# A batch norm over 32 images: tiles of half the columns in six buffers, and loads and stores that wait for their buffer alone

## The chip, the cores and the metric

The kernel runs on one core of a Trainium2 chip. The core has engines that compute, each with its own stream of instructions (here VectorE, called DVE in the profile, and ScalarE, called ACT), an engine that issues transfers (SyncE, called SP), and 16 DMA engines that move data between the chip's memory (HBM) and the core's own memory (SBUF, 128 partitions). The metric is the time of one execution on the device in microseconds (us); lower is better.

## The reference

The input x has the shape 32 x 256 x 128 x 128 (images, channels, height, width) in float32, 537 MB. The four parameters have one number per channel.

```python
def reference(x, gamma, beta, running_mean, running_var):
    eps = 1e-5
    mean = running_mean.reshape(1, -1, 1, 1)
    var = running_var.reshape(1, -1, 1, 1)
    gamma = gamma.reshape(1, -1, 1, 1)
    beta = beta.reshape(1, -1, 1, 1)
    return gamma * (x - mean) / np.sqrt(var + eps) + beta
```

Per channel this is one multiplication and one addition for every element: out = scale * x + shift, with scale = gamma / sqrt(var + eps) and shift = beta - mean * scale.

## The kernel before

The 256 channels are two blocks of 128, one channel to a partition. A tile is one image and one channel block: 128 partitions x 16384 columns (HW), 64 KB in each partition, 8.39 MB in all. There are 64 tiles (NT), and the list `order` (L84) takes all images of the first channel block and then all of the second. Three buffers `t0` to `t2` (NBUF) hold a tile each; tile i uses buffer i mod 3, and the result is written over the input in the same buffer.

**Start.** SP issues the left half of tile 0 (L87, semaphore `early`), the four parameter rows (L90), the right half of tile 0 (L94) and tiles 1 and 2 (L96). VectorE transposes the parameter rows so that each channel's number lies in its own partition (L107, L112), and ScalarE and VectorE work out `scale_t` and `shift_t` (L114 to L124).

**Loads.** For tiles 3 to 63 SP waits until the tile that had the buffer is stored (L102), and then for one more thing: `vdone` must have reached 2(i - 1) + 1, which is when VectorE has done the first small part of tile i - 1. That second wait (L104) is attached to the load itself (L103). So at most one load is in flight, since VectorE's first part waits for tile i - 1 to land.

**Compute.** VectorE takes the columns up to VCOLS = 14336 with one instruction `tensor_scalar` per part (L129): first STEP = 2560 columns, whose end lets the next load go, and then the other 11776. ScalarE takes the last 2048 columns with an `activation` (L140). For the last tile the border is VLAST = 9216.

**Stores.** ScalarE's stream has, for each tile, a wait for VectorE's two parts of it, then its own part, which also waits until the store of the tile before has ended, and then the store of the whole tile, issued from ACT's DMA queue (L153) once its own part is done (`adone`). So one store is in flight at a time.

At the end SP waits for the last stores and clears the semaphores (L171, L172).

Of the kernel before, what the change touches and what calls it, by code (L numbers as in the profile page):

```python
# [6 lines left out]


NBUF = 3
PAD = 936  # L10


STEP = 2560
VCOLS = 14336
VLAST = 9216


@with_exitstack
def kernel(
    ctx: ExitStack,  # L20
    tc: tile.TileContext,
    x: bass.AP,
    gamma: bass.AP,
    beta: bass.AP,
    running_mean: bass.AP,
    running_var: bass.AP,
    out: bass.AP,
):
    nc = tc.nc
    eps = 1e-5  # L30
    f32 = mybir.dt.float32

    N, C, H, W = x.shape
    P = nc.NUM_PARTITIONS
    assert C % P == 0
    NCB = C // P
    HW = H * W
    NT = N * NCB
    B = 32
    NQ = P // B  # L40
    NE = 16
    NPAR = 4

    xr = x.rearrange("n (cb p) h w -> (n cb) p (h w)", p=P)
    outr = out.rearrange("n (cb p) h w -> (n cb) p (h w)", p=P)

    def tile_of(name, *shape):
        return nc.alloc_sbuf_tensor(name, list(shape), f32)

    rows = tile_of("rows", B, NPAR * C)  # L50
    turned = tile_of("turned", B, NPAR * C)
    par = tile_of("par", P, NPAR, NCB)
    eps_t = tile_of("eps_t", P, 1)
    std_t = tile_of("std_t", P, NCB)
    rstd_t = tile_of("rstd_t", P, NCB)
    scale_t = tile_of("scale_t", P, NCB)
    ms_t = tile_of("ms_t", P, NCB)
    shift_t = tile_of("shift_t", P, NCB)
    tile_of("pad", P, PAD)
    bufs = [tile_of(f"t{s}", P, HW) for s in range(NBUF)]  # L60

    names = [f"loaded{s}" for s in range(NBUF)] + [f"stored{s}" for s in range(NBUF)]
    names += ["early", "vdone", "adone", "fetched", "vec", "act"]
    sems = {name: nc.alloc_semaphore(name) for name in names}
    loaded = [sems[f"loaded{s}"] for s in range(NBUF)]
    stored = [sems[f"stored{s}"] for s in range(NBUF)]
    early, vdone, adone, fetched, vec, act = (sems[n] for n in names[2 * NBUF :])
    used = range(min(s.num for s in sems.values()), max(s.num for s in sems.values()) + 1)
    assert len(used) == len(sems)

    count = [0]

    def step(inst, sem=None, value=None):
        if sem is not None:
            inst._wait_ge(sem, value)
        elif count[0]:
            inst._wait_ge(vec, count[0])
        inst.then_inc(vec, 1)
        count[0] += 1
        return count[0]  # L80

    left, right = slice(0, HW // 2), slice(HW // 2, HW)
    last = NT - 1
    order = [n * NCB + cb for cb in range(NCB) for n in range(N)]  # L84

    with tc.tile_critical():  # L86
        nc.sync.dma_start(out=bufs[0][:, left], in_=xr[order[0]][:, left]).then_inc(early, 16)  # L87
        zeroed = step(nc.vector.memset(rows[:], 0.0))  # L88
        for r, ap in enumerate((running_var, gamma, beta, running_mean)):
            inst = nc.sync.dma_start(out=rows[0:NE, r * C : (r + 1) * C], in_=ap.partition_broadcast(NE))  # L90
            if r == 0:
                inst._wait_ge(vec, zeroed)
            inst.then_inc(fetched, 16)
        nc.sync.dma_start(out=bufs[0][:, right], in_=xr[order[0]][:, right]).then_inc(loaded[0], 16)  # L94
        for i in range(1, NBUF):
            nc.sync.dma_start(out=bufs[i][:], in_=xr[order[i]]).then_inc(loaded[i], 16)  # L96
    tc.close()
    tc.compile()  # L98

    for i in range(NBUF, NT):  # L100
        s, turn = i % NBUF, i // NBUF
        nc.sync.wait_ge(stored[s], 16 * turn)  # L102
        inst = nc.sync.dma_start(out=bufs[s][:], in_=xr[order[i]]).then_inc(loaded[s], 16)  # L103
        inst._wait_ge(vdone, 2 * (i - 1) + 1)  # L104

    step(nc.vector.memset(eps_t[:], eps))  # L106
    step(nc.vector.transpose(out=turned[:], in_=rows[:]), fetched, 16 * NPAR)  # L107

    blocks = turned[:].rearrange("p (rc q b) -> p rc q b", q=NQ, b=B)
    flat = par[:].rearrange("p r cb -> p (r cb)")  # L110
    for q in range(NQ):
        placed = step(nc.vector.tensor_copy(out=flat[q * B : (q + 1) * B], in_=blocks[:, :, q, 0]))  # L112
    var_t, gamma_t, beta_t, mean_t = (par[:, r] for r in range(NPAR))
    nc.scalar.activation(  # L114
        out=std_t[:],
        in_=var_t,
        func=mybir.ActivationFunctionType.Sqrt,
        bias=eps_t[:],
        scale=1.0,
    )._wait_ge(vec, placed).then_inc(act, 1)  # L120
    step(nc.vector.reciprocal(out=rstd_t[:], in_=std_t[:]), act, 1)  # L121
    step(nc.vector.tensor_mul(out=scale_t[:], in0=gamma_t, in1=rstd_t[:]))  # L122
    step(nc.vector.tensor_mul(out=ms_t[:], in0=mean_t, in1=scale_t[:]))  # L123
    ready = step(nc.vector.tensor_sub(out=shift_t[:], in0=beta_t, in1=ms_t[:]))  # L124
    nc.vector.wait_ge(vec, ready)

    def vector_part(i, first, end):
        t, cb = bufs[i % NBUF], order[i] % NCB
        return nc.vector.tensor_scalar(  # L129
            out=t[:, first:end],  # L130
            in0=t[:, first:end],
            scalar1=scale_t[:, cb : cb + 1],
            scalar2=shift_t[:, cb : cb + 1],
            op0=mybir.AluOpType.mult,
            op1=mybir.AluOpType.add,
        ).then_inc(vdone, 1)

    def scalar_part(i, first):
        t, cb = bufs[i % NBUF], order[i] % NCB
        return nc.scalar.activation(  # L140
            out=t[:, first:],
            in_=t[:, first:],
            func=mybir.ActivationFunctionType.Identity,
            bias=shift_t[:, cb : cb + 1],
            scale=scale_t[:, cb : cb + 1],
        ).then_inc(adone, 1)

    def landed(i):
        return loaded[i % NBUF], 16 * (i // NBUF + 1)

    def store(i):
        s = i % NBUF
        nc.scalar.dma_start(out=outr[order[i]], in_=bufs[s][:])._wait_ge(adone, i + 1).then_inc(stored[s], 16)  # L153

    vector_part(0, 0, HW // 2)._wait_ge(early, 16)
    vector_part(0, HW // 2, VCOLS)._wait_ge(*landed(0))
    for i in range(1, NT):
        vector_part(i, 0, STEP)._wait_ge(*landed(i))
        vector_part(i, STEP, VLAST if i == last else VCOLS)
    for i in range(last):  # L160
        nc.scalar.wait_ge(vdone, 2 * (i + 1))
        inst = scalar_part(i, VCOLS)
        if i:
            inst._wait_ge(stored[(i - 1) % NBUF], 16 * ((i - 1) // NBUF + 1))
        store(i)
    scalar_part(last, VLAST)._wait_ge(*landed(last))
    nc.scalar.wait_ge(vdone, 2 * NT)
    store(last)

    for s in range(NBUF):  # L170
        nc.sync.wait_ge(stored[s], 16 * ((NT - s + NBUF - 1) // NBUF))  # L171
    nc.sync.sem_clear(used)  # L172
# [30 lines left out]
```

## Time and profile before

| what | value |
|---|---|
| time, median of 3 runs | 2481.03 us (2480.61 to 2481.18) |
| the profiled execution's own time | 2480.81 us |
| its span in the profile | 2479.5 us |
| VectorE busy | 508.7 us, 139 instructions |
| ScalarE busy | 139.8 us, 66 instructions |
| moved to and from HBM | 536.94 MB read, 536.87 MB written, 433 GB/s over the span |
| a tile's load, issue to landing (median) | 37.0 us |
| a tile's store, issue to landing (median) | 36.5 us |
| VectorE, 11776 columns / 2560 columns | 6406 ns / 1612 ns |
| ScalarE, 2048 columns | 2092 ns |

The span is the time from the first to the last instruction that the profiler recorded; the execution's own time has a little around it. Busy time is the sum of an engine's instruction durations. A DMA is a transfer; it is cut into packets, and each packet runs on one of the 16 DMA engines. Queue q1 carries SP's transfers (loads), q10 those of ACT (stores). The share of the DMA engines is the sum of the packets' durations over 16 engines and the length of the stretch, where a packet is counted in the stretch in which it starts; in a very short stretch the share is therefore far above 1.

### The profile page before, as it was taken

What the parts mean: (1) busy time and instruction counts of PE and PEld (TensorE: products, weight loads), DVE (VectorE), ACT (ScalarE), POOL (GpSimd) and SP (SyncE); (2) the same over time, 40 slices, a digit from 0 to 9 for tenths busy, and PEclk for the clock granted to TensorE, in tenths of its full rate; (3) what the DMA queues carried; (4) which work ended last, traced back from release to release, by engine and by line L of the source; (5) the groups of instructions that cost most, each with busy time, mean ns of one, the idle gap of its engine ahead of it and who ended that gap; (6) DMA issues with size and microseconds to landing.
All of it is one profiled execution on the core that took longest, in us unless ns stands there. A gap on an engine that the chain in (4) does not pass through costs nothing.

```text
span 2479.5 us, 514 instructions
## 1 busy us (share of the span) xinstructions
DVE 508.7 (21%) x139; ACT 139.8 (6%) x66; POOL 0.2 (0%) x4
## 2 busy tenths in 40 slices
DVE  2122121221212212122121221212212122121220
ACT  0000000000000000000000000000000000000001
POOL 0000000000000000000000000000000000000000
DMA  9999999999999999999999999999999999999999
GB/s 412 435 438 427 437 438 429 436 438 429 435 438 430 435 439 430 433 438 433 431 438 432 432 438 432 432 438 432 432 438 433 431 438 433 431 438 435 430 438 410
DMA packets 18708, 1073.85 MB, mean 433 GB/s; under 512 B 2128, under 2 KB 2192, under 8 KB 2192
## 3 DMA queue, kind: packets, MB, share of 16 engines
q1 hardware_dynamic: 9488, 536.94, 50.1%
q10 hardware_dynamic: 9216, 536.88, 50.0%
q14 instruction: 4, 0.03, 0.0%
HBM read 536.94 MB, written 536.87 MB: 433 GB/s over the span
## 4 chain that ended last, share of the span: by engine, by line
DMA 92%; DVE 4%; another core or an unknown queue 2%; ACT 0%; issue 0%; SPq 0%; DVEq 0%
DMA t<-in_x_dram 92%; DVE t L129 4%; ACT t L140 0%; SPq L90 0%; DVE rows L88 0%; DVEq L98 0%; SPq L86 0%
## 5 line engine op out<-in xcount | busy, mean ns | idle before, releaser
L129 DVE TENSOR_SCALAR t<-t,scale_t,shift_t 128x11776 f32<-128x11776 f32 (+2 forms) x128 | 505.2, 3989 | 1928.4 <-DMA t<-in_x_dram 1928.3
L140 ACT ACTIVATE t<-t,shift_t,scale_t 128x2048 f32<-128x2048 f32 x64 | 138.2, 2159 | 2297.3 <-DMA out_dram<-t 2274.5
L107 DVE STREAM_TRANSPOSE turned<-rows 32x1024 f32<-32x1024 f32 x1 | 1.2, 1232 | 7.6 <-DMA rows<-in_running_mean_dram 7.6
L114 ACT ACT_TABLE_LOAD x1 | 1.3, 1283 | 6.4 <-PEq L98 6.4
L88 DVE MEMSET rows<- 32x1024 f32 x1 | 0.9, 912 | 1.2 <-SPq L86 1.2
L106 DVE MEMSET eps_t<- 128x1 f32 x1 | 0.1, 59 | 4.4 <-PEq L98 4.4
L114 ACT ACTIVATE std_t<-par,eps_t 128x2 f32<-128x2 f32 x1 | 0.3, 295 | 8.5 <-DVE par L112 8.5
L112 DVE COPY par<-turned 32x8 f32<-32x8 f32 x4 | 0.7, 162 | 0.1
L121 DVE RECIPROCAL rstd_t<-std_t 128x2 f32<-128x2 f32 x1 | 0.2, 165 | 0.4 <-ACT std_t L114 0.4
L122 DVE TENSOR_TENSOR scale_t<-par,rstd_t 128x2 f32<-128x2 f32 x1 | 0.2, 161 | 0.0
L123 DVE TENSOR_TENSOR ms_t<-par,scale_t 128x2 f32<-128x2 f32 x1 | 0.2, 161 | 0.0
L124 DVE TENSOR_TENSOR shift_t<-par,ms_t 128x2 f32<-128x2 f32 x1 | 0.2, 160 | 0.0
L187 POOL MEMSET const-bfloat16-1.0<- 128x1 bf16 x1 | 0.1, 101 | 0.0
L187 POOL MEMSET const-uint8-127<- 128x1 uint8 x1 | 0.1, 101 | 0.0
L187 POOL MEMSET const-float32-0.0<- 128x1 f32 x1 | 0.1, 98 | 0.2 <-issue 0.2
L187 POOL MEMSET const-float32-1.0<- 128x1 f32 x1 | 0.1, 98 | 0.0
## 6 DMA issues: line engine op xcount, KB each, us to landing
t<-in_x_dram SPq DMA_DIRECT2D x2, 4096.0 KB, 16.0
out_dram<-t ACTq DMA_DIRECT2D x64, 36.5
t<-in_x_dram SPq DMA_DIRECT2D x63, 37.0
rows<-in_running_var_dram SPq DMA_DIRECT2D x1, 16.0 KB, 11.2
rows<-in_gamma_dram SPq DMA_DIRECT2D x1, 16.0 KB, 11.0
rows<-in_beta_dram SPq DMA_DIRECT2D x1, 16.0 KB, 10.7
rows<-in_running_mean_dram SPq DMA_DIRECT2D x1, 16.0 KB, 10.7
```

Of the source, the lines that this page charges most:

```text
L88: zeroed = step(nc.vector.memset(rows[:], 0.0))
L106: step(nc.vector.memset(eps_t[:], eps))
L107: step(nc.vector.transpose(out=turned[:], in_=rows[:]), fetched, 16 * NPAR)
L112: placed = step(nc.vector.tensor_copy(out=flat[q * B : (q + 1) * B], in_=blocks[:, :, q, 0]))
L114: nc.scalar.activation(out=std_t[:], in_=var_t, func=mybir.ActivationFunctionType.Sqrt, bias=eps_t[:], scale=1.0,)._wait_ge(vec, placed).t ...
L121: step(nc.vector.reciprocal(out=rstd_t[:], in_=std_t[:]), act, 1)
L122: step(nc.vector.tensor_mul(out=scale_t[:], in0=gamma_t, in1=rstd_t[:]))
L123: step(nc.vector.tensor_mul(out=ms_t[:], in0=mean_t, in1=scale_t[:]))
L124: ready = step(nc.vector.tensor_sub(out=shift_t[:], in0=beta_t, in1=ms_t[:]))
L129: return nc.vector.tensor_scalar(out=t[:, first:end], in0=t[:, first:end], scalar1=scale_t[:, cb : cb + 1], scalar2=shift_t[:, cb : cb + 1 ...
L140: return nc.scalar.activation(out=t[:, first:], in_=t[:, first:], func=mybir.ActivationFunctionType.Identity, bias=shift_t[:, cb : cb + 1] ...
L187: nc = _bacc.Bacc("TRN2", target_bir_lowering=False, num_devices=1)
```

## The change

A tile is split into two half tiles of 8192 columns (SPLIT = 2, COLS), so there are 128 half tiles, in six buffers of 32 KB per partition, as much memory as before. The order is: all images of the first channel block, with the left half and then the right half of each, then the second block.

SP issues half tile 0, the parameter rows and half tiles 1 to 5, and then a load for each further half tile as soon as the store of the half tile that had its buffer has ended; the wait for VectorE's first part is gone. VectorE has one instruction for each half tile, 7168 columns (4608 for the last), which waits for the load. ScalarE takes the other 1024 (3584) columns; its instruction waits for the load as well, no longer for VectorE and no longer for the store before. Between ScalarE's part and the store there is now a wait for VectorE's part. Ahead of its first part ScalarE waits once for the parameters.

```diff
-NBUF = 3
+SPLIT = 2
+NBUF = 3 * SPLIT
...
-STEP = 2560
-VCOLS = 14336
-VLAST = 9216
+VCOLS = 7168
+VLAST = 4608
...
-    NT = N * NCB
+    COLS = HW // SPLIT
+    NT = N * NCB * SPLIT
...
-    bufs = [tile_of(f"t{s}", P, HW) for s in range(NBUF)]
+    bufs = [tile_of(f"t{s}", P, COLS) for s in range(NBUF)]
...
-    order = [n * NCB + cb for cb in range(NCB) for n in range(N)]
+    order = [(n, cb, h) for cb in range(NCB) for n in range(N) for h in range(SPLIT)]
+
+    def part_of(ap, i):
+        n, cb, h = order[i]
+        return ap[n * NCB + cb][:, h * COLS : (h + 1) * COLS]
+
+    def load(i):
+        s = i % NBUF
+        return nc.sync.dma_start(out=bufs[s][:], in_=part_of(xr, i)).then_inc(loaded[s], 16)
...
-        nc.sync.dma_start(out=bufs[0][:, left], in_=xr[order[0]][:, left]).then_inc(early, 16)
+        load(0)
...
-        nc.sync.dma_start(out=bufs[0][:, right], in_=xr[order[0]][:, right]).then_inc(loaded[0], 16)
         for i in range(1, NBUF):
-            nc.sync.dma_start(out=bufs[i][:], in_=xr[order[i]]).then_inc(loaded[i], 16)
+            load(i)
...
     for i in range(NBUF, NT):
-        s, turn = i % NBUF, i // NBUF
-        nc.sync.wait_ge(stored[s], 16 * turn)
-        inst = nc.sync.dma_start(out=bufs[s][:], in_=xr[order[i]]).then_inc(loaded[s], 16)
-        inst._wait_ge(vdone, 2 * (i - 1) + 1)
+        load(i)._wait_ge(stored[i % NBUF], 16 * (i // NBUF))
...
-        nc.scalar.dma_start(out=outr[order[i]], in_=bufs[s][:])._wait_ge(adone, i + 1).then_inc(stored[s], 16)
+        nc.scalar.dma_start(out=part_of(outr, i), in_=bufs[s][:])._wait_ge(adone, i + 1).then_inc(stored[s], 16)
 
-    vector_part(0, 0, HW // 2)._wait_ge(early, 16)
-    vector_part(0, HW // 2, VCOLS)._wait_ge(*landed(0))
-    for i in range(1, NT):
-        vector_part(i, 0, STEP)._wait_ge(*landed(i))
-        vector_part(i, STEP, VLAST if i == last else VCOLS)
-    for i in range(last):
-        nc.scalar.wait_ge(vdone, 2 * (i + 1))
-        inst = scalar_part(i, VCOLS)
-        if i:
-            inst._wait_ge(stored[(i - 1) % NBUF], 16 * ((i - 1) // NBUF + 1))
+    for i in range(NT):
+        vector_part(i, 0, VLAST if i == last else VCOLS)._wait_ge(*landed(i))
+    nc.scalar.wait_ge(vec, ready)
+    for i in range(NT):
+        scalar_part(i, VLAST if i == last else VCOLS)._wait_ge(*landed(i))
+        nc.scalar.wait_ge(vdone, i + 1)
         store(i)
-    scalar_part(last, VLAST)._wait_ge(*landed(last))
-    nc.scalar.wait_ge(vdone, 2 * NT)
-    store(last)
```

## The prediction

> **What bounds the kernel now.** I read four views: the page, the waits of the DMA queues, the chain of waits, and busy time in stretches of the span. From the page:
>
> ```profile
> span 2479.5 us, 514 instructions
> DVE 508.7 (21%) x139; ACT 139.8 (6%) x66; POOL 0.2 (0%) x4
> ...
> DMA packets 18708, 1073.85 MB, mean 433 GB/s; under 512 B 2128, under 2 KB 2192, under 8 KB 2192
> ...
> q1 hardware_dynamic: 9488, 536.94, 50.1%
> q10 hardware_dynamic: 9216, 536.88, 50.0%
> ...
> DMA 92%; DVE 4%; another core or an unknown queue 2%; ACT 0%; issue 0%; SPq 0%; DVEq 0%
> ```
>
> VectorE (DVE) works a fifth of the time, ScalarE (ACT) a sixteenth. The two DMA queues, q1 (loads, from SP) and q10 (stores, from ACT), together keep the 16 DMA engines 100.1% occupied. The packets tell how: q10 has 9216 = 64 stores x (128 + 16), so a store is 128 packets of one 64 KB row each, and 16 short ones that raise the semaphore, one per engine. An engine thus moves 8 rows of each load and 8 of each store: 16 rows per tile, 1024 in all. The last line, the chain that ended last, is 92% transfers and names the loads, since SP issues each when the one before has landed.
>
> The pacing shows in the waits of SP's queue and in the landings:
>
> ```profile
> SPq L102 <- DMA out_dram<-t: 1395.0, 61, 66.0
> SPq L103 <- DVE t L129: 984.8, 61, 16.5
> ...
> 206.02 36.97 DMA t<-in_x_dram
> ...
> 2369.72 37.33 DMA t<-in_x_dram
> ```
>
> The load at 206.02 takes 36.97 us. The tile period is (2369.72 - 206.02) / 56 = 38.638 us, so for 1.67 us of every period no load is issued. Does an engine stand idle then? These stretches say no (last columns: busy share of the 16 DMA engines, GB/s):
>
> ```profile
> 75.00:2440.00 2365.00, 484.02 (x122) 127.63 (x61) 0.00 (x0) 1.00 1.00 434
> 30.00:75.00 45.00, 7.93 (x2) 2.09 (x1) 0.00 (x0) 1.00 1.01 431
> 13.79:13.80 0.01, 0.00 (x0) 0.00 (x0) 0.00 (x0) 1.00 7.58 3277
> 21.05:21.06 0.01, 0.01 (x1) 0.00 (x0) 0.00 (x0) 1.00 7.58 3277
> 22.26:22.27 0.01, 0.00 (x0) 0.00 (x0) 0.00 (x0) 1.00 15.17 6554
> 29.51:29.52 0.01, 0.00 (x0) 0.00 (x0) 0.00 (x0) 1.00 15.11 6554
> 1207.61:1207.62 0.01, 0.00 (x0) 0.00 (x0) 0.00 (x0) 1.00 0.06 0
> 2476.62:2476.63 0.01, 0.00 (x0) 0.00 (x0) 0.00 (x0) 1.00 15.11 6554
> ```
>
> The first row has share 1.00: while the load queue waits, the stores have the engines, and the reverse. So the waits that the change removes (984.8 us on SP, 2274.5 us on ACT for the store before) cost nothing today.
>
> The last six rows catch single packets: a stretch of 0.01 us counts what starts in it, so 3277 GB/s is one packet of 32 KB and 6554 one of 64 KB (15.17 for it holds one short packet more), and the share x 16 x 0.01 is how long its record lasts. 64 KB: 15.11 x 0.16 = 2.418 us. 32 KB (the first tile is loaded in halves): 7.58 x 0.16 = 1.213. A semaphore packet: 0.06 x 0.16 = 0.009. Records overlap a little, since the shares add up to over 100%. The true cadence of 64 KB is from the period: two semaphore packets taken off (0.011), 38.627 / 16 = 2.4142 us. A record is thus some 0.0035 too long.
>
> One engine then needs 1024 x 2.4142 = 2472.1 us for rows and, with 64 + 65 + 4 semaphore packets at 0.009 - 0.0035 = 0.0055, 0.7 more. The first packet is seen at 1.95 us, nothing before it. That is 2474.8 of the 2479.5. **The end is set by the DMA engines' occupancy, and only 4.7 us lie outside it** (the start of the first transfers, small parameter rows, the entry of the first store, the slowest engine's stalls, 0.4 us at the end).
>
> **The change, part by part.**
>
> *Rows cut in two.* Bytes are the same, but every 64 KB row becomes two packets of 32 KB: 1024 packets more per engine. What does a second packet cost? Below: nothing, if 32 KB took half of 2.4142. By records: 2 x 1.213 - 2.418 = 8 ns. With the overlap taken off each record: 2 x 1.2095 - 2.4142 = 4.8 ns. By cadence: the same engine starts 32 KB packets at 13.79 and 21.05, six steps on, so 1.2100 each (within 0.0017), and 2 x 1.2100 - 2.4142 = 5.8 ns. I take 5 ns, between the last two: 1024 x 5 = **5.1 us**, bounds 0 and 8.2. No 32 KB store is in this trace; 64 KB rows keep the cadence with both queues mixed, so I give stores the same price. It lies on the path: engines have no free time to hide it.
>
> The Trainium skill, page "DMA: Bandwidth & Descriptors", section "Why small descriptors are slow", puts a fixed overhead of about 3 cycles on each packet, at 32 bytes a cycle. At this trace's 65,536 bytes in 2.414 us, 96 bytes take 3.5 ns, an estimate from that page, and 1024 of them 3.6 us: by the rule the time would be 2485.1, by the rows 2486.6.
>
> *Twice the DMAs.* 128 loads and 128 stores and 4 parameter rows are 260 semaphore packets per engine for 133: 127 x 0.0055 = **0.7 us** (bounds 0 and 127 x 0.009 = 1.1). Issue costs 0.33 us on SP and 0.34 on ACT each, 128 each in 2480 us, while earlier transfers run: nothing.
>
> *Waits removed on SP (store alone is left) and ACT (the store before).* Gain 0 by the 1.00 share. What the cover needs: that an engine always has a row queued. A half tile's period is half of 38.6, 19.3 us plus a little. A buffer goes round in six of these, 116 us, and is out of both queues only for compute, issues and start: VectorE's 7168 columns from the rows of 8192 (4547 ns) and 6656 (3741), 0.525 ns a column, 4.0 us; ScalarE's 1024 beside it, from 2048 (2092) and 7168 (6362), 1.2 us; two issues 0.7; two starts at 1.0 (issue 0.95, first packet 1.95), or 3.6 each at worst. 7 to 12 us of 116: five of six buffers stand in a queue. If that cover went, each half tile would lay bare those 7 us.
>
> *The wait for the two parts, before the store.* Behind it on ACT stand that store and the next ScalarE part; VectorE is done 2.8 us after ScalarE, so each store leaves up to 2.8 us late, out of that 116. ACT's new wait for the parameters ends at 17.34 us, with the loads on the engines.
>
> *Head and tail.* SP issues the same bytes in the same order up to the parameters; first store at about 17.5 + 4.0 = 21.5 instead of 29.09, with loads queued either way: nothing. At the end the last half tile computes for (16384 / 2 - 4608) = 3584 columns of ScalarE, 3.4 us, where it was 6.36 under a store still running; now two or three half stores are queued before it, 4.19 MB at 434 GB/s = 9.7 us each. Nothing.
>
> **Sum:** 2479.5 + 5.1 + 0.7 = 2485.3 us of span. The profiled execution took 2480.81, 1.3 above its span and 0.2 under the median shown: **2486.6 us**, 5.6 over the median 2481.03, 0.22%.
>
> **Rivals.**
>
> *Not slower.* The second packet of a row is free, its set-up done while the other queue's packet moves, and the engines, no longer started together by a wait for all 16, lose some of the 4.7 us to stalls no more. For it: no mixed 32 KB traffic is shown. Against: loads alone, before the first store, stepped 22.26 to 29.51 in three, 2.417 each (within 0.003), as the mix does with 2.4142, so alternation hides nothing there. Price: +0.7 and -4.7 to 0, so 2476.8 to 2481.5, say 2480. It decides if a 32 KB packet in the mix steps by under 1.2075.
>
> *Contention of deep queues.* Several loads and stores stand queued at once, reads and writes collide where the pacing kept one of each. The only such stretch here is 30 to 75 us, loads queued ahead against the first store: 431 GB/s, though part of that is its entry. At 431 throughout, 2480.8 x 434 / 431 = 2498, with the packets 2504.
>
> *The queues run dry together.* Loads wait for stores alone; if all six buffers are computed at one time, 7 us lie bare once per six half tiles, 128 / 6 x 7 = 149 us: 2636. Against: the 116 us account.
>
> *A fixed price per DMA.* If the 1.67 us gap of a queue were bare for the 128 DMAs more, 214 us: 2700. The share of 1.00 through 61 such gaps speaks against it. The same page, "Two cost components", gives a fixed cost of about 2 us per DMA; 128 would be 256 us by it, an estimate, and the trace sides with cover.
>
> **Numbers.** A change under 0.2% (5 us) can hardly be told from none here, and the forecast lies just over it. Forecast 0.60 (of it 0.44 over the bound, 0.16 under); not slower 0.18 (0.03 faster by over 0.2%, which even all of the 4.7 us would hardly give); contention 0.14; dry 0.05; price per DMA 0.03. Slower 0.44 + 0.14 + 0.05 + 0.03 = 0.66, same 0.16 + 0.15 = 0.31, faster 0.03. The likeliest's own range is 2481.5 (packets free) to 2490.1 (records' 8.2 + 1.1). To hold 8 in 10 I reach down to 2480 and up to 2500: left out are dry, price per DMA, half of contention and a quarter of not slower.
>
> **What would show it.** Right: data packets doubled, the share still 1.00 in every middle stretch, 432 to 433 GB/s there, 32 KB packets in the mix 1.2095 apart. Wrong: stretches of share under 1.00 (dry), 32 KB records well over 1.213 (contention), or a middle rate still of 434 and more (free).

## The result, and the profile after

The changed kernel takes 2559.55 us (median of 4 runs, 2555.07 to 2571.43). The kernel before took 2480.87 us on the same chip (2480.61 to 2481.18). The ratio is 1.032, with an interval of 1.031 to 1.034: 79 us slower, where 5.6 were forecast and 2500 was the upper end of the range. The profiled execution is the one of 2555.07 us, so its span of 2553.8 us is compared with 2479.5 us: 74.3 us more.

The page of the changed kernel (busy time, GB/s in 40 slices, queues with their share of the 16 DMA engines, the chain, two groups of instructions, the issues):

```profile
span 2553.8 us, 712 instructions
DVE 515.8 (20%) x139; ACT 162.5 (6%) x130; POOL 0.2 (0%) x4
...
GB/s 411 421 424 429 424 424 428 426 426 425 425 427 428 425 425 423 423 427 424 425 427 423 421 423 422 422 424 421 420 422 422 423 421 423 420 423 424 421 423 302
DMA packets 36997, 1073.86 MB, mean 421 GB/s; under 512 B 4160, under 2 KB 4224, under 8 KB 4224
...
q1 hardware_dynamic: 18560, 536.94, 50.7%
q10 hardware_dynamic: 18432, 536.88, 48.8%
...
another core or an unknown queue 78%; DVE 20%; DMA 1%; issue 0%; ACT 0%; SPq 0%; ACTq 0%; DVEq 0%
...
L133 DVE TENSOR_SCALAR t<-t,scale_t,shift_t 128x7168 f32<-128x7168 f32 x128 | 512.3, 4002 | 2006.3 <-DMA t<-in_x_dram 2006.2
L144 ACT ACTIVATE t<-t,shift_t,scale_t 128x1024 f32<-128x1024 f32 x128 | 161.0, 1258 | 2359.1 <-DMA t<-in_x_dram 2358.2
...
t<-in_x_dram SPq DMA_DIRECT2D x128, 4096.0 KB, 76.7
out_dram<-t ACTq DMA_DIRECT2D x128, 4096.0 KB, 38.5
```

Bytes are the same, data packets are doubled (18432 = 128 stores x (128 + 16)), and the engines that compute have plenty of room: each half tile waits for its load. A load lies 76.7 us between issue and landing, nearly four half tile periods of 20.0 us, so several loads stand queued. But the rate in the middle is 420 to 429 GB/s, and it falls in the course of the run. The last slice has 302. The same row of the kernel before, where the mean from 75 to 2440 us was 434, ends with 410:

```profile
GB/s 412 435 438 427 437 438 429 436 438 429 435 438 430 435 439 430 433 438 433 431 438 432 432 438 432 432 438 432 432 438 433 431 438 433 431 438 435 430 438 410
```

The chain of waits is no help here: SP and ACT no longer release one transfer by another, and the chain puts 78% down to a queue it can't name.

Busy time in stretches of the changed kernel (last columns: share of the 16 DMA engines, GB/s):

```profile
500.00:1000.00 500.00, 100.33 (x25) 31.02 (x25) 0.00 (x0) 1.00 1.00 426
1000.00:1500.00 500.00, 100.31 (x25) 31.02 (x25) 0.00 (x0) 1.00 1.00 424
1500.00:2000.00 500.00, 103.41 (x26) 32.26 (x26) 0.00 (x0) 1.00 1.00 422
2000.00:2400.00 400.00, 81.17 (x21) 24.82 (x20) 0.00 (x0) 1.00 1.00 422
2489.00:2553.80 64.80, 10.70 (x3) 5.86 (x3) 0.00 (x0) 1.00 0.72 304
```

The reader should see two losses. In the middle the engines are never idle (share 1.00) and yet move less: each packet's record must be longer. In the last 65 us they are idle for 28% of the time in the mean, which is 18 us.

The packets themselves, read from the trace, say which are longer. (The trace doesn't name a packet's engine. Packets of one engine follow each other with an overlap of 3 to 4 ns in their records, and by this they were strung together.) The mean record of a load packet is 1.262 us, of a store packet 1.215, where a 32 KB packet undisturbed takes 1.213. Sorted by place within its transfer's eight packets on one engine, this is the excess over 1.213 us:

```
mean excess in ns, by place:       1    2    3    4    5    6    7    8
changed kernel, loads, 600-1000  186   61   15   12    6    4    3    4
changed kernel, loads, 1800-2200 334  111   19   12    9    3    3   10
changed kernel, stores, 600-1000   1    0    0    0    0    2    2   14
```

The first two packets of a load are the long ones, more so as the run goes on. Meanwhile the engines drift apart. A transfer raises its semaphore 16 times, once from each engine, and the time from the first to the last of these grows for loads from 0.5 us at the start to 7 (at 374 us), 21 (at 721), 45 (at 1176) and 55 us from 1400 us on, with some engines ahead by almost three half tiles: at 1800 us seven engines land a load within 2.5 us of each other, one 23 us behind the first of them and eight 43 to 54 us behind. In the kernel before these times stay at 4.5 to 4.9 us from the fifth load on. So the tail is plain too: the engines that are ahead have their part of the last load at 2478 us, the last engine at 2533. Stores are issued only when a load has landed on all 16, so the engines ahead stand idle between the last stores.

The account of the 74.3 us is this. Load and store records add up to 1292.6 + 1244.5 us per engine; in a kernel of equal bytes with clean 32 KB packets (`e6_no_pacing_rows_in_two` below) to 1243.8 + 1242.1. The difference is 51.2 us. The idle end is 18. That kernel's span is 4.0 above the kernel before, the price of the packets; with the forecast's 0.7 for semaphore packets the sum is 73.9.

### The profile page after: what moved, and what is told of

Read it like the earlier page. It is cut to its first block, busy times and chain, and to the rows that moved or that the text cites. A ratio compares the mean times of both kernels' runs of the same rounds, so it can differ in the third digit from the quotient of the medians.

```text
span 2553.8 us, 712 instructions
## 1 busy us (share of the span) xinstructions
DVE 515.8 (20%) x139; ACT 162.5 (6%) x130; POOL 0.2 (0%) x4
## 2 busy tenths in 40 slices
DMA packets 36997, 1073.86 MB, mean 421 GB/s; under 512 B 4160, under 2 KB 4224, under 8 KB 4224
## 3 DMA queue, kind: packets, MB, share of 16 engines
q10 hardware_dynamic: 18432, 536.88, 48.8%
## 4 chain that ended last, share of the span: by engine, by line
another core or an unknown queue 78%; DVE 20%; DMA 1%; issue 0%; ACT 0%; SPq 0%; ACTq 0%; DVEq 0%
DVE t L133 20%; DMA t<-in_x_dram 1%; ACT t L144 0%; SPq L98 0%; DVE rows L96 0%; SPq L92 0%; ACTq L157 0%; DVEq L105 0%; ACTq L164 0%; SPq L94 0%
## 5 line engine op out<-in xcount | busy, mean ns | idle before, releaser
L133 DVE TENSOR_SCALAR t<-t,scale_t,shift_t 128x7168 f32<-128x7168 f32 x128 | 512.3, 4002 | 2006.3 <-DMA t<-in_x_dram 2006.2
L144 ACT ACTIVATE t<-t,shift_t,scale_t 128x1024 f32<-128x1024 f32 x128 | 161.0, 1258 | 2359.1 <-DMA t<-in_x_dram 2358.2
## 6 DMA issues: line engine op xcount, KB each, us to landing
t<-in_x_dram SPq DMA_DIRECT2D x128, 4096.0 KB, 76.7
```

The source lines that it names most:

```text
L133: return nc.vector.tensor_scalar(out=t[:, first:end], in0=t[:, first:end], scalar1=scale_t[:, cb : cb + 1], scalar2=shift_t[:, cb : cb + 1 ...
L144: return nc.scalar.activation(out=t[:, first:], in_=t[:, first:], func=mybir.ActivationFunctionType.Identity, bias=shift_t[:, cb : cb + 1] ...
```

## The experiments

Unless said otherwise an edit is made to the changed kernel. Times are medians, ratios are against the kernel before on the same chip (2480.8 to 2481.2 us).

### Which half of the change costs it: the waits or the half tiles

First theories: **A**, transfers that stand queued behind others have longer packets, so a wait before each brings the time back; **D**, the loss is the drift, and a wait for all 16 engines ends it; **B**, half tiles are slow by themselves.

`e1_loads_paced`: each load also waits for the load before to land.

```diff
-        load(i)._wait_ge(stored[i % NBUF], 16 * (i // NBUF))
+        nc.sync.wait_ge(stored[i % NBUF], 16 * (i // NBUF))
+        load(i)._wait_ge(loaded[(i - 1) % NBUF], 16 * ((i - 1) // NBUF + 1))
```

> The changed kernel, but a load is also issued only when the half tile before it has landed; stores as in the change. Theory A (queued behind: a load that stands in the queue behind another load has long first packets, +140 to +334 ns for the first and +55 to +111 for the second in the changed kernel, none in the kernel before): no load is queued behind another any more, so its first packets go back to 1.213 us and the span to 2484 to 2490 us. Theory D (drift: the 16 engines go out of step because no wait for all of them stands between one transfer and the next on a queue, and out of step they hinder each other): the same, 2484 to 2490, since the load's wait is for all 16. Theory B (the half rows of 32 KB, 64 KB apart, are slow to load by themselves): stays over 2535.

Measured: 2671.11 us, ratio 1.075 (1.073 to 1.077). The engines are in step (mostly 2 to 6 us apart), but load packets are longer still, 145 ns over 1.213 us in the mean (200 to 2400 us). A and D miss; by its number B holds.

`e2_full_tiles_no_pacing`: no waits, whole tiles.

```diff
-SPLIT = 2
+SPLIT = 1
...
-VCOLS = 7168
-VLAST = 4608
+VCOLS = 14336
+VLAST = 9216
```

> The changed kernel with whole tiles (64 KB rows) in three buffers, no pacing. Theory A: half as many loads, and with three buffers only some of them stand behind another one: 64 boundaries at 0.2 to 0.45 us are 13 to 29 us, span 2490 to 2512. Theory D: drift as in the change, over 2520, with the 16 semaphore packets of one load spread over tens of us. Theory B: 2477 to 2483, as the kernel before.

Measured: 2497.95 us over 10 runs that reach from 2480.87 to 2518.22, ratio 1.005 (1.002 to 1.007). The span of the profiled run, 2498.0, lies in the range of A; B's is below it and D's above it. Without waits, whole tiles drift too: one engine falls 18 us (loads) and 30 us (stores) behind the first, the other 15 stay within 5 to 8 us. Most of the loss is in the last slice of this page's GB/s:

```profile
GB/s 421 436 426 430 437 434 437 430 433 428 432 431 436 436 428 433 425 434 436 436 432 436 434 428 437 436 434 434 436 433 429 437 436 436 433 436 433 429 437 311
```

The middle holds 434, the end has 311. While the engine falls behind, up to some 1400 us, the first packet of a load is longer here too (85 ns in the mean of 64 KB packets at 600 to 1000 us); from 1800 us on the engine is as far behind as before and load packets are clean, 0.1 ns over 2.418 us. So one engine that is behind costs a tail and not the rate.

`e3_stores_paced`: each ScalarE part waits for the store before, as it once did.

```diff
     for i in range(NT):
+        if i:
+            nc.scalar.wait_ge(stored[(i - 1) % NBUF], 16 * ((i - 1) // NBUF + 1))
         scalar_part(i, VLAST if i == last else VCOLS)._wait_ge(*landed(i))
```

> The changed kernel, but ScalarE's part of a half tile, and so its store, waits until the store of the half tile before has ended; loads as in the change. Theory A: loads still stand behind loads, so 2540 to 2575. Theory D: the wait for all 16 engines of a store brings the engines into step again, so under 2500. Theory B: over 2535.

Measured: 2915.4 us, ratio 1.175 (1.173 to 1.177). Only B's "over 2535" allows it, and no theory had its size. Its queues and two stretches:

```profile
q1 hardware_dynamic: 18560, 536.94, 49.7%
q10 hardware_dynamic: 18432, 536.88, 42.6%
```

```profile
500.00:1000.00 500.00, 88.28 (x22) 27.31 (x22) 0.00 (x0) 1.00 0.92 366
1000.00:1500.00 500.00, 86.03 (x22) 26.06 (x21) 0.00 (x0) 1.00 0.93 368
```

The share is 0.92. A load takes 20.3 us from issue to landing here and a store 21.5, both less than the period. So all buffers are loaded by the time that a store ends, and its end releases the next store and, by its buffer, the next load; both queues are empty at once. Of a period of 500 / 22 = 22.7 us 7 to 8% are some 1.7 us idle; eight load packets that are 200 ns longer in the mean make 1.6. Together 3.3 us for each half tile; (2917.0 - 2484.5) / 128 is 3.4 (2484.5 is the span of half tiles at their best, below).

`e4_half_both_paced`: both edits. Both waits of the kernel before, with half tiles.

> The changed kernel with both waits: a load waits for the landing of the half tile before, a store for the store before. All of A and D: 2479.5 plus the price that the prediction gave the second packet of a row (5.1 us, bounds 0 and 8.2) and the semaphore packets (0.7): 2485.3 us of span, 2480 to 2489. Theory B: over 2535.

Measured: 2633.88 us, ratio 1.063 (1.060 to 1.065). In stretches:

```profile
500.00:1000.00 500.00, 99.62 (x25) 30.98 (x25) 0.00 (x0) 1.00 0.99 410
1000.00:1500.00 500.00, 97.01 (x25) 29.74 (x24) 0.00 (x0) 1.00 0.99 408
```

The share is 0.99 and the rate 408: again records are longer, this time those of stores, 1.302 us in the mean. The excess sits at their first, fourth and fifth packet (265, 269 and 247 ns at 600 to 1000 us), and at the first of a load (132 ns).

A and D (2480 to 2489) miss, B (over 2535) holds. So the first verdict is a table of spans, one profiled run each, and the waits aren't the cause: with half tiles, taking them away **gains** 79 us. It is the half tile that costs, either way.

| span, us | both waits | neither |
|---|---|---|
| whole tiles | 2479.5 (before) | 2498.0 (e2) |
| half tiles | 2633.2 (e4) | 2553.8 (the change) |

### Is it the length of a packet or the number of transfers

**L**: a 32 KB packet is too short to cover the start of the next transfer, 64 KB is not. **N**: it is the number of transfers.

`e5_paced_rows_in_two` keeps whole tiles and all waits of the kernel before, and stores the two halves of a row 64 B apart in the buffer, so that every packet has 32 KB. The edit, to the kernel before:

```diff
+GAP = 8
...
-    bufs = [tile_of(f"t{s}", P, HW) for s in range(NBUF)]
+    bufs = [tile_of(f"t{s}", P, HW + 2 * GAP) for s in range(NBUF)]
...
+    def halves(ap):
+        return ap.rearrange("p (h c) -> p h c", h=2)
+
+    def buf(i):
+        return halves(bufs[i % NBUF][:])[:, :, 0 : HW // 2]
...
-        inst = nc.sync.dma_start(out=bufs[s][:], in_=xr[order[i]]).then_inc(loaded[s], 16)
+        inst = nc.sync.dma_start(out=buf(i), in_=halves(xr[order[i]])).then_inc(loaded[s], 16)
```

> The kernel before, whole tiles, both its waits, as many DMAs, but the two halves of a row lie 64 bytes apart in the buffer, so that each row is two packets of 32 KB (VectorE has three parts for two). Theory L (a transfer's first packets start late, and one packet of the other queue that is on the engine meanwhile covers the start if it lasts 2.4 us, not if it lasts 1.2): 64 loads and 64 stores lose what a half tile lost with both waits, (2633.2 - 2485.3) / 128 = 1.16 us each time: 2485 + 64 x 1.16 = 2559, at least 2520. Theory N (the number of transfers and how often a queue runs empty decides, not the packet): only the second packet's price, 2484 to 2490.

Measured: 2505.25 us, ratio 1.010 (1.008 to 1.011), between the theories. The first packet of a store is 137 ns longer in the mean (200 to 2400 us), the seventh 81, the sixth 58.

`e6_no_pacing_rows_in_two`: the same edit to `e2_full_tiles_no_pacing`.

> Whole tiles in three buffers without pacing, rows as two packets of 32 KB (the kernel without pacing of whole tiles, 2498.0 of span, with only the packets cut). Theory L: loads keep long first packets to the end of the run, while with 64 KB they ended about halfway; 2515 to 2560. Theory N: 2485 to 2510, and the long packets end about halfway.

Measured: 2485.32 us in 10 runs (2484.78 to 2485.54), ratio 1.002 (1.001 to 1.003). In stretches:

```profile
500.00:1000.00 500.00, 103.16 (x26) 27.22 (x13) 0.00 (x0) 1.00 1.00 433
2000.00:2400.00 400.00, 79.36 (x20) 20.95 (x10) 0.00 (x0) 1.00 1.00 433
```

L falls: packets of 32 KB, reads and writes mixed and no waits run at 433 GB/s to the end, with engines 2 us apart. No packets are long from 200 us on, so N's "the long packets end about halfway" missed too, and the span is a little under its range. 1024 packets more cost 2483.5 - 2479.5 = 4.0 us, 3.9 ns each (4.3 by the medians). The Trainium skill, page "DMA: Bandwidth & Descriptors", section "Why small descriptors are slow", states a fixed overhead of about 3 cycles for each packet; the forecast's estimate from it was 3.5 ns, and the run agrees to 0.4 ns.

`e7_loads_in_two`: whole tiles, no waits, each load as two transfers of half the columns. `e8_stores_in_two`: the same for stores.

```diff
+        first = nc.sync.dma_start(out=bufs[s][:, :half], in_=part_of(xr, i)[:, :half]).then_inc(loaded[s], 16)
+        nc.sync.dma_start(out=bufs[s][:, half:], in_=part_of(xr, i)[:, half:]).then_inc(loaded[s], 16)
```

```diff
+        for cols in (slice(0, HW // 2), slice(HW // 2, HW)):
+            nc.scalar.dma_start(out=part_of(outr, i)[:, cols], in_=bufs[s][:, cols]).then_inc(stored[s], 16)
```

> Whole tiles in three buffers without pacing; each load is two DMAs of half the columns (32 KB packets), each store one DMA of 64 KB packets. Theory L: the store packet beside a starting load lasts 2.4 us and covers it: few long load packets, 2480 to 2515, although there are 128 loads. Theory N: 128 loads, as many starts as in the change, over 2530.

> The mirror: loads whole (64 KB packets), each store two DMAs of 32 KB packets, three buffers, no pacing. Theory L: the store packet beside a starting load lasts 1.2 us and does not cover it: long first load packets to the end, 64 starts, 2510 to 2550. Theory N: 64 loads, 2485 to 2515.

Measured: 2617.32 us, ratio 1.056 (1.054 to 1.058), for loads in two; 2483.85 us, ratio 1.001 (1.000 to 1.002), for stores in two. Half stores are harmless and cost their packets. Half loads alone cost more than the whole change: the load records are 52 us per engine too long, as in the change, and with them the records of the 64 KB stores, 2.503 us in the mean for 2.418, another 43 us. This fits N, if it is the loads that count, and also **H**: that it matters which addresses a load reads, half rows with gaps of 32 KB.

### Number or addresses of the loads

`e9_contiguous_halves`: a half tile is 64 channels on two partitions each, so that it reads 4.19 MB without gaps, in as many transfers and packets as the change.

```diff
-    xr = x.rearrange("n (cb p) h w -> (n cb) p (h w)", p=P)
+    xr = x.rearrange("n (ct p) (s h) w -> (n ct) (p s) (h w)", p=P // SPLIT, s=SPLIT)
...
-        return ap[n * NCB + cb][:, h * COLS : (h + 1) * COLS]
+        return ap[(n * NCB + cb) * SPLIT + h]
```

> The changed kernel (six half buffers, no pacing, 128 loads and 128 stores of 32 KB packets), but a half tile is 4.19 MB without a gap in HBM: 64 channels, each on two partitions, in place of 128 channels' half rows 64 KB apart. VectorE and ScalarE still take the parameters of 128 channels, so each channel is scaled with another channel's numbers. Theory H (what is slow is where the loads read: half rows, 32 KB of every 64 KB): as the whole tiles in two packets without pacing (2483.5), plus 0.7 us of semaphore packets: 2482 to 2492. Theory N (the number of loads, each start of which costs): 2540 to 2575 as the change.

Measured: 2495.55, 2540.03, 2498.13 and 2543.69 us. The runs fall into two groups, and no ratio can be given for both; the lower one lies above the range of H, the upper one at the lower end of that of N. More below.

`e10_contiguous_quarters`: the same with a quarter of a tile (SPLIT 4, 12 buffers, VCOLS 3584, VLAST 2304), 256 loads and 256 stores.

> The same with quarters: twelve buffers of 16 KB rows, 256 loads and 256 stores of 2.1 MB without a gap (32 channels, each on four partitions, scaled with other channels' numbers). Theory H: only packets: 4.0 us for the first doubling as measured (2483.5 - 2479.5), 12 for both, and 383 semaphore packets more, 2.1: 2489 to 2499. Theory N: 256 starts, 2600 or more.

Measured: 2498.94 us (2498.79 to 2499.1), ratio 1.007 (1.006 to 1.009), with clean packets at 431 GB/s. N falls, H holds: twice as many transfers again, and the loss is gone but for the packets.

`e11_left_halves_first`: the change with all left halves ahead of all right ones, so that loads that follow each other are of different images.

```diff
-    order = [(n, cb, h) for cb in range(NCB) for n in range(N) for h in range(SPLIT)]
+    order = [(n, cb, h) for cb in range(NCB) for h in range(SPLIT) for n in range(N)]
```

> The changed kernel with another order: for a channel block all images' left halves, then all images' right halves, so that loads and stores in flight are in the same half of their rows. Theory H, if loads and stores hinder each other by address: well over the change, 2600 or more, or at least away from it by over 20 us. If only loads hinder each other, or theory N: 2545 to 2575, as the change.

Measured: 2553.99, 2556.86, 2557.29 and 2605.85 us; the ratio of the first three is 1.030 (1.028 to 1.032), as the change. Which half comes next in the order doesn't bring the time back.

`e12_contiguous_both_paced`: `e9_contiguous_halves` with both waits of `e4_half_both_paced`.

> Half tiles without a gap in HBM (each channel scaled with another's numbers) with both waits, a load for the landing of the one before and a store for the store before. Theory H: the loss of half rows with both waits (2633.2) is gone: 2484 to 2510. Theory N: 2600 to 2650.

Measured: 2640.07 us, ratio 1.065 (1.063 to 1.067), in the range of N, as with half rows. With the waits, the gap doesn't matter.

`e13_column_quarters`: the change with SPLIT 4, 12 buffers, VCOLS 3584, VLAST 2304; quarter rows by columns, with larger gaps than the change has.

> The changed kernel with quarters by columns: twelve buffers, 16 KB rows 64 KB apart, 256 loads and 256 stores, no pacing. Its twin with quarters that have no gap in HBM took 2497.5 of span. Theory H (loads that read only a part of every 64 KB hinder each other): worse than halves by columns, over 2575. If the halves without a gap were faster by chance alone (their runs go from 2495 to 2544): 2495 to 2545.

Measured: 2498.95 us (2498.75 to 2499.66), ratio 1.007 (1.006 to 1.009). In stretches:

```profile
500.00:1000.00 500.00, 109.46 (x51) 41.53 (x51) 0.00 (x0) 1.00 1.01 431
2000.00:2400.00 400.00, 87.99 (x41) 33.38 (x41) 0.00 (x0) 1.00 1.01 431
```

431 from one end to the other, so H falls as well: gaps alone don't do it. The finer cut is 60 us faster than the change, and its 18.3 us over the span before come to 5.3 ns for each of the 3072 data packets and 383 semaphore packets that an engine has more.

`e15_quarters_both_paced`: `e10_contiguous_quarters` with both waits.

> The quarters without a gap in HBM (2497.5 unpaced; scaled with other channels' numbers) with both waits, a load for the landing of the one before, a store for the store before. Theory S (each time that a queue has to start from empty beside the other one costs 0.4 to 0.6 us, whatever the size): 512 starts for the 256 of the halves, which lost 2637.8 - 2484.2 = 154 us: 2497.5 + 307 = 2800, 2700 to 2950. If pacing costs a share of the time and not a piece per start: about 2650.

Measured: 2687.63, 2689.31, 2727.92 and 2742.96 us; the ratio of the first three is 1.089 (1.083 to 1.095). The profiled run is the one of 2689.31. The waits cost 2688.0 - 2497.5 = 190 us of span for 512 transfers, 0.37 us each, and for halves (e12) 2637.8 - 2484.5 = 153 us for 256, 0.60 each. Its span of 2688.0 lies between the two expectations: neither a constant price per start nor a constant share of the time. The Trainium skill, page "DMA: Bandwidth & Descriptors", "Two cost components", gives some 2 us fixed for a transfer, in its account of transfers that GpSimd issues; here SP and ACT issue them, and e12 and e15 lay bare a third of that or less, even with one transfer in flight in each queue.

### Do the engines slow down because they are out of step

`e16_contiguous_halves_again` is `e9_contiguous_halves` once more, with more runs.

> The halves without a gap in HBM, unpaced, once more, since its four runs lay at 2495, 2498, 2540 and 2544. Theory H: the two groups again, both under the change's 2555 to 2571, and where the profile is of the slow group, the engines are apart by tens of us from early on. If the two kinds of halves differ by chance only: runs over 2555 among them.

Measured: 2485.83, 2495.67, 2496.31, 2497.27 and 2547.76, 2548.47, 2549.54 us. With e9 that makes 6 runs of 11 at 2486 to 2498 and 5 at 2540 to 2550; the ratio of the lower group here is 1.005 (1.003 to 1.007). One program goes either way. The two experiments happen to have a profile of each. GB/s of the lower group's (e9), then of the upper group's (e16):

```profile
GB/s 413 428 436 429 436 429 436 429 436 430 435 432 434 434 431 434 432 435 429 436 430 436 429 437 429 435 432 434 431 435 434 431 435 431 434 432 435 429 437 360
```

```profile
GB/s 410 428 431 427 431 428 428 428 427 430 427 428 428 429 425 425 425 425 424 424 425 426 424 425 425 424 426 419 423 421 424 419 421 426 421 421 422 423 423 302
```

The second goes the way of the changed kernel's row, from 428 to 431 in its first slices down to 419 to 426, with the same 302 at the end, and its loads drift the same way: 0.6, 14 (at 487 us), 37 (at 1060), 54 us. In the first they are 2 to 13 us apart, and load packets have an excess of 1 to 3 ns from 200 us on. H's expectation of two groups holds. The change and e11 went adrift in 8 of 8 runs, by their times (2554 to 2606 us).

`e14_realigned`: the change, with a wait for the load before at every 16th load.

```diff
+        nc.sync.wait_ge(stored[i % NBUF], 16 * (i // NBUF))
+        if i % 16 == 0:
+            nc.sync.wait_ge(loaded[(i - 1) % NBUF], 16 * ((i - 1) // NBUF + 1))
+        load(i)
```

> The changed kernel, but every 16th load waits for the landing of the one before, so that the 16 engines cannot come further apart than 16 half tiles let them. Theory D2 (being out of step makes the packets long): long packets nearly go, 2485 to 2505. Theory H with drift as a consequence: the spread of a load's 16 semaphore packets stays under 10 us, the idle engines of the last 65 us (28% of them, 18 us) are saved, the long packets stay at the 40 ns per load packet of the changed kernel's first 400 us: 2479.5 + 4.7 + 41 + 0 to 10 = 2525 to 2535. If neither: 2545 to 2575.

Measured: 2512.87 us (2509.2 to 2524.44), ratio 1.014 (1.012 to 1.016), between the two expectations. GB/s:

```profile
GB/s 409 424 423 428 424 430 434 432 434 432 432 433 432 431 399 431 432 431 433 420 434 433 431 432 417 429 431 433 433 417 432 430 434 434 419 435 432 430 434 411
```

Seven waits hold the loads within 13 us of each other. Between the dips the rate is 430 to 434, and the tail is gone (411). 2553.8 - 2507.9 = 46 us come back, 35 of them by shorter records. Some long packets stay, 17 ns in the mean of all load packets instead of 49.

`e17_pushed_out_of_step`: `e13_column_quarters`, with two early loads split unevenly over the engines, to put loads out of step from there on.

```diff
+        if i in PUSHED:
+            first = nc.sync.dma_start(out=bufs[s][0:120], in_=part_of(xr, i)[0:120]).then_inc(loaded[s], 16)
+            nc.sync.dma_start(out=bufs[s][120:P], in_=part_of(xr, i)[120:P]).then_inc(loaded[s], 16)
+            return first
```

> The quarters by columns (2497.8 of span, engines in step, no long packets) with one push: the loads of quarter tiles 24 and 25 are split into partitions 0 to 119 and 120 to 127, so that 8 of the 16 engines get 16 rows of each and the other 8 none. That puts the two groups 20 to 40 us apart at some 250 us of the run, and gives 8 engines 16 rows of 0.6 us more in all, 10 us. Theory D (out of step is the cause): long first packets of the loads from there on, and the rate in the rest falls as in the changed kernel (434 to 424 GB/s, 2 to 3% of 2250 us): 2540 to 2570. If drift only follows from something in the halves: the 10 us of more rows and up to 10 us of idle engines at the end, 2505 to 2518, packets as short as before the push.

Measured: 2506.12 us (2505.92 to 2506.43), ratio 1.010 (1.008 to 1.012). The push was not the one that was expected. The load queue has 14 semaphore packets more than in e13 (4174 and 4160), so each of the two loads in parts has 23 in place of 16, which fits 15 engines for the 120 partitions and 8 for the rest. So a single engine was left out: from some 260 us on it lands a load 18 to 20 us ahead of the other 15, which stay within 4 us of each other at first and within 8 at the end. From first to last it is 23 to 26 us. The stretches are as clean as without the push:

```profile
500.00:1000.00 500.00, 109.45 (x51) 41.53 (x51) 0.00 (x0) 1.00 1.01 431
1000.00:1500.00 500.00, 111.53 (x52) 42.35 (x52) 0.00 (x0) 1.00 1.01 431
```

From 600 us on no place in a load shows an excess over 1 ns; around the push (200 to 600 us) records are longer, 5 us per engine in all. So one engine out of step makes no packet long in this kernel. Two groups of eight, by which theory D was to be tested and which the changed kernel comes near, were not tried, and D stays open for them.

`e18_pushed_and_realigned`: the same, with one wait at load 36 that brings the loads together again.

> The same push, and then one load (tile 36) that waits until the load before it has landed on all 16 engines. Theory D: the engines are in step again after it, the rate comes back to 431 to 432 GB/s: 2503 to 2520. If one wait does not bring them into step: as the pushed kernel without it.

Measured: 2507.00 us, ratio 1.011 (1.009 to 1.012): no better. Loads are 0.7 to 4.8 us apart again, stores 19 to 23, again by one engine. Since the push had cost no rate, there was none to bring back, and the two expectations can't be told apart.

### What is settled and what stays open

Settled: the waits that the change removes aren't the loss; half tiles with them are slower by 79 us. Not the cause, each by itself: packets of 32 KB (e6), many loads (e10, e13), half stores (e8), gaps in what is read (e13), one engine out of step (e17, and e2 from 1800 us on). The loss has two parts that go together, long first packets of loads and engines that drift, and waits that cut the drift take most of both away (e14). Such a wait also leaves the load queue empty for a moment, so e14 alone doesn't show that the drift is what mattered.

Open is why loads of eight packets per engine, in six buffers, fall into this course, in 8 of 8 runs with half rows and in 5 of 11 with contiguous halves, while quarter tiles (e10, e13) and whole tiles with rows in two (e6) don't, and whole tiles with whole rows (e2) do in a milder form. One row of the changed kernel's trace points at a loop. At 200 to 500 us the first packet of a load has an excess of 1 ns in the mean on engines that start the load within 1 us of the first engine, and of some 390 ns on those that start it over 2 us behind; in e11 it is 2 and 490. An engine that is late is thus held up further. But in the lower group of e9, and in e14 from 500 us on, engines over 2 us behind show 1 ns or less. So lateness alone doesn't do it, no run here shows the mechanism, and drift of many engines as the cause of the long packets is neither shown nor excluded. Engines in step don't protect by themselves either: with waits, in e1 and e3, packets are long though the engines are 0.4 to 7 us apart. Whole, half and quarter tiles also differ in buffers (3, 6, 12), and other numbers of buffers for half tiles weren't tried. No version tried beats the kernel before; the nearest without waits are e8 (2483.85) and e6 (2485.32).

## Why the prediction was wrong

**What bounds the kernel** was right and still holds: the DMA engines' occupancy, with the compute terms at 4.002 and 1.258 us for the 4.0 and 1.2 forecast.

**Rows cut in two**, 5.1 us: right. Measured by itself it is 4.0 (e6), inside the bounds of 0 and 8.2. With **twice the DMAs** the forecast was 2486.6 (2486.8 if the 0.2 us between the profiled execution and the median, which the sum names, is added). The best run of contiguous halves, of which no profile was kept, came to 2485.83 (e16). So the sum's terms fit half tiles when nothing else happens, though half rows never ran that way.

**"Waits removed on SP (store alone is left) and ACT (the store before). Gain 0 by the 1.00 share"** is the step that failed. The cover that it asked for was there, as the account of five buffers in six said: the share is 1.00 through the middle, and nothing ran dry. What failed is the reading of the share, and with it the 0.7 us for twice the DMAs, since by the table of four halving the tiles without waits costs 56 us. A packet that takes 1.5 us instead of 1.2 counts as busy as well, and the step assumed that a record's length is a constant of its size. The profile before shows it only for one load and one store in flight at a time, and e6 shows that it can hold without the waits. In the changed kernel load records came to 1.262 us in the mean instead of 1.213, which with the little on stores is 51 us. What lengthens them is open, as said above.

**Tail, "Nothing"** failed for 18 us. The step counted how many half stores are queued at the end. It did not ask whether the engines end together: before, with the wait for all 16 that the change removes, they were within 5 us of each other, and in the changed kernel nothing takes its place. (Whole tiles in 32 KB packets stayed within 2 us without it, in e6.)

**The wait for the two parts**, and the head: nothing was forecast. The first store is issued at 21.45 us, where 21.5 was forecast, and e6, with the same kind of wait, has only 4.0 us over the span before. Right.

**The rivals.** *Contention of deep queues* is the one that came nearest: its sign, "32 KB records well over 1.213", is what the trace shows. It was given 0.14, and priced at 2498 to 2504 from the only stretch at hand, 431 GB/s at 30 to 75 us. That stretch lay at the beginning, and the changed kernel has 421 to 424 in its second and third slice already. The price could not contain first packets that grow from 186 to 334 ns in the course of the run, nor a tail. *Not slower* held that engines no longer started together lose fewer stalls; they lose more. *Queues run dry* fell by the share of 1.00. *A fixed price per DMA* was not paid by the changed kernel, which keeps several queued; e12 and e15, with one transfer in flight in each queue, pay 0.60 and 0.37 us for each, so not a fixed one either.

One more assumption is worth naming: that the change was two edits whose costs add. The table of four says that halving costs 154 us with waits and 56 without, and that removing the waits costs 19 us with whole tiles and gains 79 with halves. The 19 is loose, since the ten runs of e2 lie 0 to 37 us over the time before.

## What to carry to other kernels

A share of 1.00 says that transfer engines are never idle, not that they move at full rate; read GB/s and the length of single packets beside it, in the profile before and at once in the one after. In a kernel bound by transfers, a wait that costs nothing may still hold 16 engines in step (within 5 us before, 18 to 30 us apart in e2), so before taking it away ask what keeps them together to the last transfer. And cut transfers and waits as separate edits: here their effects had opposite signs depending on the other, and the cut in two was worse than whole and than the cut in four.

## What the runs showed of the hardware that was not expected

- The engines of one transfer may drift 55 us apart and stay there, and one program may or may not do so: 2486 to 2498 us or 2540 to 2550 us from the same instructions (e9, e16).
- In a kernel that drifts, the first packet of a load is long on the engines that start it late (390 ns over 1.213 us for those over 2 us behind, 1 ns for those within 1 us of the first, in the changed kernel at 200 to 500 us); in the lower group of e9, and in e14 from 500 us on, late engines have clean packets.
- Long packets are bound to places: first and second of a load without waits (up to 334 and 111 ns), first, fourth and fifth of a store with both waits (265, 269, 247 ns), first, third and fourth of a load with waits for stores (576, 767, 315 ns).
- The wait for one transfer at a time, free on transfers of 8.39 MB in 64 KB packets (2479.5 us of span), cost 21 us on the same transfers in 32 KB packets (2504.3 for e5, 2483.5 for e6), 153 us at 4.19 MB and 190 us at 2.1 MB.
- Reads and writes mixed hold 434 GB/s on one core in the kernel before (75 to 2440 us), and 3.9 to 5.3 ns are lost for each further packet (e6, e13).
